# Gathering rows in fp32 and casting them on ScalarE in a gather, cumulative sum and matmul kernel

## The chip, the cores and the metric

The kernel runs on one core of one Trainium2 chip. The metric is the time of one execution on the device, in microseconds; less is better. Before the change it was 410.53 us, the median of three runs (409.6 to 411.24).

The runs of this study fell on several chips, and that turned out to matter. I call them A (the first measurement; which chip it was is not recorded; before takes 410), B (e1, e2, e3, e5 and e9 to e12; before takes 405), C (e4, e6, e7, e8; before takes 411) and D (e13 to e18; before takes **365**). A may be C. The trace of before was taken in an execution of 404.57 us, which fits B's runs of before (404.3 to 407.1 us) and not A's; its chip isn't recorded. Every ratio compares kernels of the same chip.

## The reference

```python
B, S, N, D = 16, 4096, 2048, 512
# x: B x S x D fp32; indices: B x N, sorted, without repeats; w: D x D fp32
gathered = x[b_idx, indices, :]
cs = np.cumsum(gathered, axis=1)
return np.matmul(cs, w).astype(np.float32)
```

## The kernel before

256 tiles of 128 gathered rows run through five stages. GpSimd issues an indirect DMA for a tile. TensorE multiplies the tile with a triangle of ones (`sums`, into `pa`), which gives the sums within the tile, transposed. VectorE adds the last column of the tile before (`carry`, from `pa` to `cst`). TensorE multiplies by w (`project`, into `pb`), ScalarE copies the product to an output buffer (`drain`, from `pb` to `ob`), and a DMA stores it. The lines from the helper that issues a gather:

```python
    NG = 16        # buffers for gathered tiles, R = 2 tiles in one
    def gather(t):
        g, r = divmod(t, R)
        if t % FREE == 0:
            pool.need(s_a, t + FREE - NG)     # TensorE's sums of tile t-16 (and the next) are done
        ...                                   # choose the column of indices
        nc.gpsimd.indirect_dma_start(
            out=g16[g % (NG // R)][:, r, :],  # fp16: the DMA casts
            out_offset=None,
            in_=x_flat,                       # fp32 in HBM
            in_offset=bass.IndirectOffsetOnAxis(ap=ap, axis=0),
            element_offset=(t // NT) * S * D,
        ).then_inc(s_g[t % NS], 16)
...
    for t in range(T):
        gather(t)
        if t % NB == NB - 1:                  # after each fourth tile
            nc.gpsimd.memset(rest[:, t // NB, :], 0.0)   # nobody reads it: 0.54 us of delay
```

```python
    def sums(t, u, first=None):
        ...
        pe.need(s_g[t % NS], ...)             # the tile has landed
        pe.need(s_d, t - NA + 1 - skip, tiles)  # VectorE has emptied pa
        ...                                   # 4 matmuls, then s_a += 1
    def carry(t, first=None):
        dve.need(s_a, t + 1, first)           # TensorE's sums of tile t are done
        ...                                   # add, then s_d += 1
    def drain(u, first=None):
        act.need(s_b, u + 1, first)           # TensorE's product of tile u is done
        nc.scalar.copy(out=ob[...], in_=pb[u % NB][:]).then_inc(s_e, 1)
```

## Time and profile before

| | kernel before, profiled run (404.57 us) |
|---|---|
| span, granted clock | 402.9 us, 0.937 |
| queue q0 (gathers), q1 (stores): share of 16 DMA engines | 58.2%, 43.1% |
| gathers on GpSimd | 256 of 0.94 us |
| gathers in the steady stage | one every 1.478 us |

The lines behind it stand in the prediction below. A page gives for each group the busy time, the mean of one instruction, the idle time ahead of the group on its engine and what ended most of that. A line of the waits gives who waited for what, then the sum in us, how many times, and the longest; "remote" stands where the profile found nobody who had just given the signal.

### The profile page before, as it was taken

The page shows a single profiled execution, that of the slowest core. Times are in us where ns is not written, and L with a number is a line of the kernel's source. Part 1 is how long each engine was busy: PE and PEld are TensorE (multiplying, and loading weights), DVE is VectorE, ACT ScalarE, POOL GpSimd, SP SyncE. Part 2 cuts the span into 40 slices and gives each one's busy share as a digit, 9 for nine tenths or more (in the row PEclk, how much of TensorE's full clock was granted, in tenths as well). Part 3 has the DMA queues.
Part 4 walks back from the last instruction along what each step waited for, and adds up shares of the span by engine and source line. Part 5 has one row for each costly group of instructions (what it writes and reads, how often), then busy time and mean ns, then how long its engine had stood idle before and what let it go on. Part 6 is the DMA issues. An engine that isn't in the chain of part 4 may idle for free.

```text
span 402.9 us, 6104 instructions
## 1 busy us (share of the span) xinstructions
PE 323.7 (80%) x2066; PEld 164.3 (41%) x2066; DVE 178.9 (44%) x263; ACT 144.6 (36%) x260; POOL 277.2 (69%) x330
## 2 busy tenths in 40 slices
PE   7654987978878878978887988889788897787894
PEld 2321443434434433534443434445344453343451
DVE  3311454444444544435444535444444444444561
ACT  2211343333333333333334424333333333333552
POOL 7886777777777777777677777777777767776600
PEclk9886898999999998989989898989999899989998
DMA  7988999999999999999999999999999999999985
GB/s 178 182 119 135 224 247 252 249 248 301 264 237 298 266 243 298 252 295 224 270 297 243 261 279 264 242 289 249 246 295 268 296 212 287 287 225 299 279 321 222
DMA packets 56268, 102.15 MB, mean 254 GB/s; under 512 B 5824, under 2 KB 38848, under 8 KB 56256
## 3 DMA queue, kind: packets, MB, share of 16 engines
q0 software_dynamic: 36864, 33.57, 58.2%
q1 hardware_dynamic: 18832, 67.90, 43.1%
q10 hardware_dynamic: 560, 0.53, 0.4%
q8 instruction: 6, 0.10, 0.1%
q14 instruction: 6, 0.05, 0.0%
HBM read 68.42 MB, written 67.11 MB: 336 GB/s over the span
## 4 chain that ended last, share of the span: by engine, by line
PE 76%; issue 12%; DVE 4%; another core or an unknown queue 2%; DMA 2%; POOL 2%; ACT 1%; DVEq 0%; SPq 0%
PE pb L190 58%; PE pa L145 18%; DVE cst L177 4%; POOL g L125 1%; DMA g<-in_x_dram,idxg 1%; ACT ob L202 1%; DMA idx_first<-in_indices_dram 0%; POOL rest L289 0%; DVEq L26 0%; SPq L411 0%; SPq L92 0%
## 5 line engine op out<-in xcount | busy, mean ns | idle before, releaser
L190 PE MATMUL pb<-w,cst 128*128 128x512 f16 x1024 | 284.0, 401 | 46.0 <-DVE cst L177 23.0
L125 POOL DMA_INDIRECT g<-in_x_dram,idxg x252 | 237.1, 941 | 100.6 <-issue 54.6
L177 DVE TENSOR_TENSOR cst<-pa,cst 128x512 f16<-128x512 f32 x240 | 166.0, 692 | 205.5 <-PE pa L145 163.3
L202 ACT COPY ob<-pb 128x512 f32<-128x512 f32 x256 | 142.0, 590 | 248.3 <-PE pb L190 196.8
L190 PEld LDWEIGHTS pb<-w,cst 128*128 128x128 f16 x1024 | 89.7, 102 | 126.4 <-issue 44.0
L145 PE MATMUL pa<-ut,g 128*128 128x128 f16 x992 | 106.7, 226 | 25.1 <-issue 23.7
L145 PEld LDWEIGHTS pa<-ut,g 128*128 128x128 f16 x992 | 78.0, 102 | 97.9 <-issue 45.9
L289 POOL MEMSET rest<- 128x512 f16 x64 | 34.8, 543 | 0.1
L164 DVE CAST cst<-pa 128x512 f16<-128x512 f32 x16 | 11.0, 685 | 5.5 <-PE pa L145 5.5
L296 PE MATMUL pb<-zeros 128*128 128x512 f16 x16 | 6.0, 542 | 1.5 <-DVE zeros L300 1.5
L125 POOL DMA_INDIRECT g<-in_x_dram,idx_first x4 | 3.9, 987 | 1.6 <-issue 0.9
L296 PEld LDWEIGHTS pb<-zeros 128*128 128x128 f16 x16 | 2.1, 134 | 4.3 <-issue 2.4
L145 PE MATMUL pa<-uq,g 128*128 128x128 f16 x32 | 3.1, 219 | 0.8 <-DMA g<-in_x_dram,idx_first 0.8
L145 PEld LDWEIGHTS pa<-uq,g 128*128 128x128 f16 x32 | 2.4, 97 | 2.7 <-DMA g<-in_x_dram,idx_first 1.0
L303 DVE CAST idxf<-idx 128x128 f32<-128x128 uint32 x2 | 0.5, 228 | 4.1 <-DMA idx<-in_indices_dram 4.1
L366 ACT ACT_TABLE_LOAD x1 | 1.3, 1283 | 2.6 <-issue 2.6
L369 ACT CAST w<-w 128x512 f16<-128x512 f32 x2 | 1.1, 615 | 2.6 <-DMA w<-in_w_dram 2.6
L317 DVE CAST w<-w 128x512 f16<-128x512 f32 x2 | 1.4, 748 | 0.8 <-DMA w<-in_w_dram 0.8
L308 PE MATMUL pb<-ident,idxf 128*128 128x128 f32 x2 | 0.9, 446 | 0.4 <-DVE idxf L303 0.4
L308 PEld LDWEIGHTS pb<-ident,idxf 128*128 128x128 f32 x2 | 0.4, 204 | 1.3 <-DVE idxf L303 1.0
L300 DVE MEMSET zeros<- 128x256 uint32 x1 | 0.3, 272 | 1.1 <-SPq L92 1.1
L314 DVE CAST idxg<-pb 128x128 uint32<-128x128 f32 x2 | 0.6, 288 | 0.4 <-issue 0.4
(11 smaller groups left out, 2.1 us busy)
## 6 DMA issues: line engine op xcount, KB each, us to landing
out_dram<-ob SPq DMA_DIRECT2D x62, 1024.0 KB
g<-in_x_dram,idxg POOLq DMA_INDIRECT x252
out_dram<-ob SPq DMA_DIRECT2D x4, 256.0 KB, 2.8
out_dram<-ob SPq DMA_DIRECT2D x2, 512.0 KB, 3.4
w<-in_w_dram ACTq DMA_DIRECT2D x2, 256.0 KB
w<-in_w_dram SPq DMA_DIRECT2D x2, 256.0 KB
idx<-in_indices_dram SPq DMA_DIRECT2D x2, 128.0 KB, 2.7
g<-in_x_dram,idx_first POOLq DMA_INDIRECT x4
```

Source lines behind the costliest of these rows:

```text
L125: nc.gpsimd.indirect_dma_start(out=g16[g % (NG // R)][:, r, :], out_offset=None, in_=x_flat, in_offset=bass.IndirectOffsetOnAxis(ap=ap, ax ...
L145: mm = nc.tensor.matmul(out=pa[t % NA][:, c], lhsT=g16[g % (NG // R)][:, r, c * P : (c + 1) * P], rhs=uq[:] if g in PLAIN else ut[:], star ...
L164: nc.vector.tensor_copy(out=dst, in_=src).then_inc(s_d, 1)
L177: nc.vector.tensor_tensor(out=dst, in0=src, in1=last, op=mybir.AluOpType.add).then_inc(s_d, 1)
L190: mm = nc.tensor.matmul(out=pb[u % NB][:], lhsT=cst[g % NC][:, c, j, :], rhs=w16[:, c, :], start=(c == 0), stop=(c == DC - 1),)
L202: nc.scalar.copy(out=ob[g // W % NO][:, g % W, j], in_=pb[u % NB][:]).then_inc(s_e, 1)
L289: nc.gpsimd.memset(rest[:, t // NB, :], 0.0)
L296: nc.tensor.matmul(out=pb[NB - 1][:], lhsT=zeros[:, :P], rhs=zeros[:], start=True, stop=True)
L308: nc.tensor.transpose(out=pb[k % NB][:, :P], in_=idxf[:, k, :], identity=ident[:]).then_inc(s_pt, 1)
L317: nc.vector.tensor_copy(out=w16[:, c, :], in_=w32[:, c, :]).then_inc(s_wc, 1)
L366: nc.scalar.copy(out=spare[:], in_=zeros[:, :1])
L369: nc.scalar.copy(out=w16[:, c, :], in_=w32[:, c, :]).then_inc(s_wc, 1)
```

## The change

Intent: on the DMA engines a gathered row that is cast on its way takes longer than a plain one (98 ns at the median for a cast row in the trace of before, 84 for a packet of 2 KB that isn't cast). So gather plain fp32 rows and cast on ScalarE, which is busy for 36% of the time. The clearing after each fourth gather goes. Of each 16th tile the last 8 rows are gathered by an instruction of their own, after the reset that stands in the diff. I meant this to take load off one DMA engine. The first eight pairs of tiles are stored singly.

```diff
-    LEAD = 4
+    LEAD = 3
+    FAR = 6            # casts run up to 6 tiles ahead of the drain
+    NH = 8             # fp16 buffers
...
     def gather(t):
-        if t % FREE == 0:
-            pool.need(s_a, t + FREE - NG)
+        if t >= NG:
+            pool.need(s_c, cast_by[R * (g + 1) - NG - 1])   # ScalarE has cast tile t-16
...
+        parts = [(0, P, ap, s_g[t % NG])]
+        if t % NT == SPLIT:
+            pool.need(s_last, 16)
+            nc.gpsimd.inc_swdge_sem([], [], mode="reset_dge_cursor")
+            parts = [(P - E, P, idx_last[:, t // NT, 0:1], s_h),
+                     (0, P - E, ap[: P - E], s_g[t % NG])]
+        for a, b, ap, done in parts:
+            nc.gpsimd.indirect_dma_start(out=g32[g % (NG // R)][a:b, r, :], ...)
+    def cast(t, n, first=None):
+        for u in range(t, t + n):
+            act.need(s_g[u % NG], ...)
+        nc.scalar.copy(out=g16[...], in_=g32[...]).then_inc(s_c, 1)
...
-    for g in range(W):
+    for g in range(W * NO):
         store(g, 1)
...
-        if t % NB == NB - 1:
-            nc.gpsimd.memset(rest[:, t // NB, :], 0.0)
...                                   # ScalarE's loop: casts, then the drain of tile u
+        for t, n in casts[u if first is None else 2 * U + u]:
+            cast(t if first is None else t - 2 * U, n, first)
         drain(u, first)
```

More of the change, by code (lines that the diff above doesn't have):

```diff
@@ L53 @@
     KI = T // P
+    E = 8
+    SPLIT = NT // 2
     FIRST = 2 * R
     NG = 16
-    NS = 32
-    FREE = 2
-    LEAD = 4
+    LEAD = 3
+    FAR = 6
+    NH = 8
     NA = 4
@@ L64 @@
     U = NT
-    V = NS
-    assert V % NS == 0 and NS % NG == 0 and FREE == R and NS == 16 * R and 2 * U % NS == 0 and (T - 4 * U) % V == 0 and U % (W * R * NO) == 0 and U % NA == 0 and U % (R * NC) == 0 and U % NB == 0
+    V = max(U, W * R * NO)
+    assert U == NT == NG == W * R * NO and V % U == 0 and V % (W * R * NO) == 0 and T % V == 0 and U % NG == 0 and U % NA == 0 and U % (R * NC) == 0 and U % NB == 0
     assert D == 512 and N % (R * P) == 0 and T % P == 0
@@ L74 @@
     idx_first = const.tile([P, FIRST, 2], U32)
+    idx_last = const.tile([E, B, 2], U32)
     idx64 = const.tile([P, KI, 2 * P], U32)
@@ L84 @@
     spare = const.tile([P, 1], FP16)
-    rest = const.tile([P, T // NB, D], FP16)
-    g16 = [const.tile([P, R, D], FP16, name=f"g16_{i}") for i in range(NG // R)]
+    g32 = [const.tile([P, R, D], FP32, name=f"g32_{i}") for i in range(NG // R)]
+    g16 = [const.tile([P, R, D], FP16, name=f"g16_{i}") for i in range(NH)]
     cst = [const.tile([P, DC, R, P], FP16, name=f"cst{i}") for i in range(NC)]
@@ L95, in sem @@
         return tc.alloc_semaphore(name)
-    s_z, s_ut, s_wc, s_if, s_pt, s_prep, s_of, s_c = (
-        sem(f"s_{n}") for n in ("z", "ut", "wc", "if", "pt", "prep", "of", "c")
+    s_z, s_ut, s_wc, s_if, s_pt, s_prep, s_c = (
+        sem(f"s_{n}") for n in ("z", "ut", "wc", "if", "pt", "prep", "c")
     )
@@ L102 @@
     s_idx = [sem(f"s_idx{k}") for k in range(KI)]
+    s_last = sem("s_last")
+    s_h = sem("s_h")
+    s_f = [sem(f"s_f{i}") for i in range(NO)]
     s_ol = sem("s_ol")
-    s_g = [sem(f"s_g{i}") for i in range(NS)]
+    s_g = [sem(f"s_g{i}") for i in range(NG)]
     s_o = [sem(f"s_o{i}") for i in range(NO)]
@@ L113 @@
     )
+    casts = []
+    cast_by = []
+    for u in range(T):
+        far = min(FAR, 2 if u < R else 3 + (u + 4) // 8, 3 + (T - 1 - u) // 6)
+        casts.append([])
+        while len(cast_by) <= min(u + far, T - 1):
+            n = R if far > 5 and len(cast_by) % R == 0 else 1
+            casts[u].append((len(cast_by), n))
+            cast_by += [cast_by[-1] + 1 if cast_by else 1] * n
+    for u in range(2 * U + U, T - 2 * U):
+        assert casts[u] == [(t + U, n) for t, n in casts[u - U]]
     def gather(t):
         g, r = divmod(t, R)
-        if t % FREE == 0:
-            pool.need(s_a, t + FREE - NG)
+        if t >= NG:
+            pool.need(s_c, cast_by[R * (g + 1) - NG - 1])
         if t < FIRST:
@@ L124, in gather @@
             ap = idxg[:, t // P, t % P : t % P + 1]
-        nc.gpsimd.indirect_dma_start(
-            out=g16[g % (NG // R)][:, r, :],
-            out_offset=None,
-            in_=x_flat,
-            in_offset=bass.IndirectOffsetOnAxis(ap=ap, axis=0),
-            element_offset=(t // NT) * S * D,
-        ).then_inc(s_g[t % NS], 16)
-    PLAIN = (0, 1, G - 2, G - 1)
+        parts = [(0, P, ap, s_g[t % NG])]
+        if t % NT == SPLIT:
+            pool.need(s_last, 16)
+            nc.gpsimd.inc_swdge_sem([], [], mode="reset_dge_cursor")
+            parts = [
+                (P - E, P, idx_last[:, t // NT, 0:1], s_h),
+                (0, P - E, ap[: P - E], s_g[t % NG]),
+            ]
+        for a, b, ap, done in parts:
+            nc.gpsimd.indirect_dma_start(
+                out=g32[g % (NG // R)][a:b, r, :],
+                out_offset=None,
+                in_=x_flat,
+                in_offset=bass.IndirectOffsetOnAxis(ap=ap, axis=0),
+                element_offset=(t // NT) * S * D,
+            ).then_inc(done, 16)
+    PLAIN = (0, 1, G - 2, G - 1)
+    def cast(t, n, first=None):
+        g, r = divmod(t, R)
+        for u in range(t, t + n):
+            act.need(s_g[u % NG], 16 * (u // NG + 1), first)
+            if u % NT == SPLIT:
+                act.need(s_h, 16 * (u // NT + 1), first)
+        nc.scalar.copy(
+            out=g16[g % NH][:, r : r + n], in_=g32[g % (NG // R)][:, r : r + n]
+        ).then_inc(s_c, 1)
     def sums(t, u, first=None):
@@ L138, in sums @@
         tiles = None if first is None else R * first
-        skip = 0 if first is None else 2 * U
-        pe.need(s_g[t % NS], 16 * (t // NS + 1) - skip // R, first)
-        pe.need(s_d, t - NA + 1 - skip, tiles)
+        pe.need(s_c, cast_by[t] if first is None else cast_by[2 * U + t] - 2 * U // R, first)
+        pe.need(s_d, t - NA + 1, tiles)
         for c in range(DC):
             if c == 1 and u is not None:
-                pe.need(s_e, u - NB + 1 - skip, tiles)
+                pe.need(s_e, u - NB + 1, tiles)
             mm = nc.tensor.matmul(
                 out=pa[t % NA][:, c],
-                lhsT=g16[g % (NG // R)][:, r, c * P : (c + 1) * P],
-                rhs=uq[:] if g in PLAIN else ut[:],
+                lhsT=g16[g % NH][:, r, c * P : (c + 1) * P],
+                rhs=uq[:] if first is None and g in PLAIN else ut[:],
                 start=(c == 0),
@@ L183, in project @@
         tiles = None if first is None else R * first
-        skip = 0 if first is None else 2 * U
-        pe.need(s_e, u - NB + 1 - skip, tiles)
-        pe.need(s_d, (u + 1 if g in PLAIN else R * (g + 1)) - skip, tiles)
+        pe.need(s_e, u - NB + 1, tiles)
+        pe.need(s_d, u + 1 if first is None and g in PLAIN else R * (g + 1), tiles)
         for c in range(DC):
             if c == 2 and t is not None:
-                pe.need(s_d, t - NA + 1 - skip, tiles)
+                pe.need(s_d, t - NA + 1, tiles)
             mm = nc.tensor.matmul(
@@ L206, in store @@
         rows = out[b, h * R * P : (h + n) * R * P, :]
-        src = ob[g // W % NO]
+        i = g // W % NO
+        src = ob[i]
+        done = s_ol if g >= G - W else s_f[i] if 0 < g < W * NO and g % W else s_o[i]
         if g in (0, G - 1):
@@ L210, in store @@
                 sp.need(s_e, R * g + j + 1)
-                done = s_ol if g else (s_o[0], s_of)[j]
                 nc.sync.dma_start(
                     out=rows[j * P : (j + 1) * P, :], in_=src[:, g % W, j]
-                ).then_inc(done, 16)
+                ).then_inc(s_f[0] if j and not g else done, 16)
             return
         sp.need(s_e, R * (g + n))
-        done = {1: s_of, G - W: s_ol}.get(g, s_o[g // W % NO])
+        order = "(g j p) d -> p g j d" if g in PLAIN else "(g p j) d -> p g j d"
         nc.sync.dma_start(
-            out=rows.rearrange(
-                "(g j p) d -> p g j d" if g in PLAIN else "(g p j) d -> p g j d", p=P, j=R
-            ),
-            in_=src[:, g % W : g % W + n],
+            out=rows.rearrange(order, p=P, j=R), in_=src[:, g % W : g % W + n]
         ).then_inc(done, 16)
@@ L234 @@
             ).then_inc(s_first[k], 16)
+        nc.scalar.dma_start(
+            out=idx_last[:],
+            in_=indices[:, (SPLIT + 1) * P - E : (SPLIT + 1) * P]
+            .bitcast(U32)
+            .rearrange("b (p w) -> p b w", w=2),
+        ).then_inc(s_last, 16)
     idx_rows = indices.bitcast(U32).rearrange("b (t q) -> (b t) q", q=2 * P)
@@ L242 @@
         eng.dma_start(out=w32[:, c, :], in_=w[c * P : (c + 1) * P, :]).then_inc(s_w[c], 16)
-    for g in range(W):
+    for g in range(W * NO):
         store(g, 1)
-    for g in range(W, G - W, W):
+    for g in range(W * NO, G - W, W):
         store(g, W)
@@ L341 @@
     tail = order.index((False, T - 2 * U - 1)) + 1
-    step = 2 * V
+    step = 2 * U
     for i in range(head + step, tail):
-        assert order[i] == (order[i - step][0], order[i - step][1] + V)
+        assert order[i] == (order[i - step][0], order[i - step][1] + U)
     def run(i, first=None):
@@ L348, in run @@
         after = next((v for k, v in order[i + 1 :] if k != is_sums), None)
+        if first is not None:
+            t -= 2 * U
+            after -= 2 * U
         if is_sums:
@@ L356 @@
         run(i)
-    with nc.tensor.Fori(2 * U // R, (T - 2 * U) // R, V // R) as first:
+    with nc.tensor.Fori(2 * U // R, (T - 2 * U) // R, U // R) as first:
         pe.new_pass()
@@ L371, in step @@
         if u % (W * R) == 0:
-            if first is None and u == W * R * NO:
-                act.need(s_of, 16 * (R + W - 2))
-            act.need(s_o[u // R // W % NO], 16 * (u // R // W // NO), first)
+            i, slot = divmod(u // (W * R), NO)
+            if first is None and i == 1:
+                act.need(s_f[slot], 16 * (W - 1 + (slot == 0) * (R - 1)))
+            act.need(s_o[slot], 16 * i, first)
+        for t, n in casts[u if first is None else 2 * U + u]:
+            cast(t if first is None else t - 2 * U, n, first)
         drain(u, first)
@@ L379 @@
         step(u)
-    with nc.scalar.Fori(2 * U, T - 2 * U, U) as first:
+    with nc.scalar.Fori(2 * U, T - 2 * U, V) as first:
         act.new_pass()
-        for u in range(U):
+        for u in range(V):
             step(u, first)
```

## The prediction

> **What bounds the kernel now.** I read the page first: the slices, the DMA queues, the HBM line.
>
> ```profile
> PE   7654987978878878978887988889788897787894
> POOL 7886777777777777777677777777777767776600
> DMA  7988999999999999999999999999999999999985
> q0 software_dynamic: 36864, 33.57, 58.2%
> q1 hardware_dynamic: 18832, 67.90, 43.1%
> HBM read 68.42 MB, written 67.11 MB: 336 GB/s over the span
> ```
>
> The DMA digit is 9 from the fifth slice to within 20 us of the end, and the two queues together took 101% of what 16 engines have. PE is at 7 to 9. q0 is the gathers (32768 rows and 4096 semaphore writes), q1 the stores. Next, the steady stage alone: the windows, limited to the tile g, so the POOL column counts gathers and nothing else.
>
> ```profile
> 10.00:50.00 40.00, 8.01 (x72) 6.35 (x72) 26.35 (x28) 0.79 0.88 164
> 50.00:350.00 300.00, 88.08 (x816) 63.47 (x816) 190.63 (x203) 0.95 1.06 265
> ```
>
> (Columns: window, length, PE, weight loads, POOL, each busy us and count, granted clock, DMA share, GB/s.) 203 gathers in 300 us is **1.478 us per tile** of 128 rows; 256 tiles at that rate are 378 us. The other 402.9 - 378 = 25 us is start and tail; from 10 to 50 us only 28 gathers were issued, at a lower clock and DMA share.
>
> Is it really DMA? The groups, the waits and the timeline say what the others need per tile.
>
> ```profile
> L190 PE MATMUL pb<-w,cst 128*128 128x512 f16 x1024 | 284.0, 401 | 46.0 <-DVE cst L177 23.0
> L202 ACT COPY ob<-pb 128x512 f32<-128x512 f32 x256 | 142.0, 590 | 248.3 <-PE pb L190 196.8
> L289 POOL MEMSET rest<- 128x512 f16 x64 | 34.8, 543 | 0.1
> L369 ACT CAST w<-w 128x512 f16<-128x512 f32 x2 | 1.1, 615 | 2.6 <-DMA w<-in_w_dram 2.6
> ...
> ACT ob L202 <- remote: 43.3, 22, 4.3
> POOL g L125 <- PE pa L145: 23.1, 38, 1.4
> POOL g L125 <- remote: 22.9, 17, 2.5
> ...
> 10.19 0.94 POOL L125 DMA_INDIRECT g<-in_x_dram,idxg  x1 [0.30 <-issue]
> 11.44 0.94 POOL L125 DMA_INDIRECT g<-in_x_dram,idxg  x1 [0.30 <-issue]
> 12.68 0.94 POOL L125 DMA_INDIRECT g<-in_x_dram,idxg  x1 [0.30 <-issue]
> 13.61 0.55 POOL L289 MEMSET rest<- 128x512 f16 x1
> 14.32 0.95 POOL L125 DMA_INDIRECT g<-in_x_dram,idxg  x1 [0.17 <-issue]
> 386.83 0.58 PEld L190 LDWEIGHTS pb<-w,cst 128*128 128x128 f16 x4
> 386.89 1.03 PE L190 MATMUL pb<-w,cst 128*128 128x512 f16 x4
> 387.97 1.03 PE L190 MATMUL pb<-w,cst 128*128 128x512 f16 x4
> ```
>
> POOL unhindered issues a gather every 11.44 - 10.19 = 1.245 us; with the memset after each fourth, four tiles take 14.32 - 8.94 = 5.38 us (8.94 is the start of the gather before these rows), 1.345 us each. So it is only 9% faster than the 1.478 us that the stage runs at, and it waited 46 us for buffers. PE at full clock does a tile in 387.97 - 386.89 = 1.08 us; VectorE's add takes 0.69. ACT waited 43 us for something remote: its output buffers, which stores must empty. Each engine is faster than 1.478 and held up by buffers that transfers free: **the DMA engines bound the steady stage**.
>
> The transfer records, one by one, size it. A gathered row (2 KB read, 1 KB written as fp16) takes 98 ns at the median, the semaphore write behind it 22; a 4 KB store packet 159 to 172; a 2 KB packet that isn't cast (the weights, and stores of 2 KB runs) **84**. Per tile and engine: 8 x 98 + 22 for the gather, 4 x 161 for the store, about 5 for the store's semaphores: 1.455 us, 98.4% of 1.478. Some 1,600 gather rows took 150 ns to over 1 us (the mean is 112), which is why shares add to more than one; they overlap packets of the other queue.
>
> [...]
>
> **The change, part by part.**
> Gathers in fp32: each row is a plain 2 KB packet, I take 84 ns for 98. Per tile and engine 8 x 14 = 112 ns less. HBM traffic is the same; SBUF writes double. 1.478 - 0.112 = 1.366 us per tile, times 256 = 349.7 us, **28.7 us less**. This is on the bounding resource, so it counts in full while nothing else takes more than 1.366.
>
> Casts on ACT: in the loop one instruction of 1024 columns per pair[...]; a drain is 0.59[...]. Beside other work, except at the start and the end, where a cast of 615 ns is one more link: +1 to +2 us. The order of instructions shows ACT casting six tiles ahead of its drain, and a gather waiting for the cast of the tile 16 before it, about what sums gave before.
>
> Memsets gone: POOL falls to 1.245 us per tile.
>
> Split of tile 8 of each 16: one more gather of 8 rows and one cursor reset on POOL. If these cost together 1.0 us (an estimate: the 0.30 gap[...]), 1.245 + 1.0/16 = 1.31 us per tile. Still under 1.366, barely. [...]
>
> First eight pairs stored singly: stores start earlier in a stage where the DMA has gathers only (121 and 128 GB/s from 20 to 40 us). I take 2 to 3 us off, against the added casts.
>
> Sum: 349.7 + 25 (start and tail) - 2.5 + 1.5 = 373.7, rounded down to 372.5[...]. Runs without a profile were 410.53 - 402.9 = 7.6 us longer than this span: **380 us**, 7.4% less.
>
> **The rivals.**
> (a) POOL becomes the bound. If the reset and the small gather cost 3 us and more a time[...], POOL needs 1.43 us per tile and up: 366 us + start 3 + tail 12 + 7.6 = 389. For it: POOL is within 9% now, and nothing in the trace prices the reset. Against: only 16 of them.
> (b) A 2 KB packet saves nothing beside stores: HBM reads and writes together must rise from 2 x 262144 B / 1.478 us = 355 GB/s to 384, and the write side of SBUF doubles for gathers. If rows still took 98 ns, the time would be 408. Against: 98 is the cast's own time, as weight rows of the same 2 KB took 84; and in the transfer view of 200 to 250 us single slices of 1.25 us, with stores in them, moved 401 to 410 GB/s.
> (c) ACT becomes a coupling: casts stand in order behind drains that wait for stores, and gathers wait for casts. A stall of 4 us (the longest above) then stops gathers too. Against: 16 buffers are over 20 us of gathers, and the DMA has stores to move in just those stalls. I'd give it 3 to 8 us.
> (d) The slow start shortens by far more than I take: up to 10 us, giving 370.
>
> **Range and chances.** The centre 380 has the cast saving in full; (c) and (a) in mild forms reach 390 to 396[...]. Range 368 to 396. Within 2% means over 402.3: that takes (b), or (a) in a severe form. Faster 0.91, same 0.06, slower 0.03.
>
> **What would show it.** Right: gather packets of 2 KB near 84 ns, q0's share of the engines falling from 58% to about 50% of a shorter span, gathers every 1.36 us in the steady stage, DMA still at 9[...]. Wrong: DMA below 9 with POOL's waits gone (a); rows near 98 ns (b); POOL waiting long for ACT's casts while DMA digits fall to 8 (c). The whole is wrong if a reset takes microseconds or if the stores' packets lengthen as the gathers' shorten.

The sum came to 349.7 + 25 - 2.5 + 1.5 = 373.7 us of span; I put it at 372.5 for a small gain by the split, and 7.6 us more gave 380. Of the 1.0 us for the reset and the small gather only the gap of 0.30 us is from the trace; the rest was my guess. That the casts fit beside other work can be put from the trace alone: a cast of 512 columns took 615 ns and a drain 590, so one of each per tile makes about 1.21 us, under 1.366 (an estimate).

## The result

The changed kernel took **471.25 us** (median of four runs, 467.16 to 475.28), beside 410.06 for before: ratio 1.1455 (95% interval 1.1353 to 1.1557), **slower**. The result is correct. A ratio is the mean time of one kernel's fast runs over that of the other's of the same rounds, so not quite the ratio of the medians. The profiled run of the changed kernel (475.28 us, span 473.3) counts as slow, as it lies 1.7% above the fastest; its granted clock of 0.873 is that of the fast runs (0.872 to 0.874).

The page of the changed kernel, slices and queues, to be held against those in the prediction:

```profile
PE   6408783875887687678678587587769747758595
POOL 7756556464655745566545565557566555665200
DMA  7766878787988978798878898798799888888756
q0 software_dynamic: 20992, 67.13, 44.1%
q1 hardware_dynamic: 18880, 67.90, 36.7%
HBM read 68.42 MB, written 67.11 MB: 286 GB/s over the span
```

The DMA digit fell from 9 to 7 and 8, and GpSimd's from 7 to 5 and 6. q0 did fall, from 58.2% of 403 us to 44.1% of 473: the engines have less to do, yet everything takes longer. The windows say the same of the steady stage (columns: window, length, then PE, weight loads, ACT and POOL with counts, for tile g alone; granted clock, DMA share, GB/s):

```profile
50.00:350.00 300.00, 74.01 (x692) 57.59 (x692) 92.59 (x92) 174.46 (x184) 0.87 0.84 299
```

184 gather instructions in 300 us where before had 203, some of them the small ones. Groups and waits of the changed kernel:

```profile
L154 POOL DMA_INDIRECT g<-in_x_dram,idxg x252 | 240.4, 954 | 141.4 <-issue 71.0
L154 POOL DMA_INDIRECT g<-in_x_dram,idx_last x16 | 14.4, 899 | 37.4 <-ACT g L171 33.6
L171 ACT CAST g<-g 128x1024 f16<-128x1024 f32 (+1 forms) x147 | 138.9, 948 | 0.3 <-issue 0.2
```

```profile
ACT ob L239 <- PE pb L227: 104.0, 78, 4.2
POOL g L154 <- ACT g L171: 104.1, 42, 5.2
ACT ob L239 <- remote: 82.1, 24, 11.5
```

GpSimd waits 104 us for ScalarE's casts, 42 times, up to 5.2 us at once. A gather of 8 rows takes 899 ns and one of 128 rows 954: the price is per instruction, not per row. GpSimd's timeline shows the rhythm:

```profile
212.63 0.95 POOL L154 DMA_INDIRECT g<-in_x_dram,idxg  x1 [0.30 <-issue]
213.89 0.95 POOL L154 DMA_INDIRECT g<-in_x_dram,idxg  x1 [0.30 <-issue]
215.14 0.95 POOL L154 DMA_INDIRECT g<-in_x_dram,idxg  x1 [0.31 <-issue]
217.87 0.95 POOL L154 DMA_INDIRECT g<-in_x_dram,idxg  x1 [1.78 <-ACT g L171]
```

Several gathers at 1.25 us each, then a pause; the one shown ended when a cast did. ScalarE's timeline there, from TensorE's signal on: a drain, then the cast, which ends at 217.60 us.

```profile
216.07 0.59 ACT L239 COPY ob<-pb 128x512 f32<-128x512 f32 x1 [2.00 <-PE pb L227]
216.55 1.05 ACT L171 CAST g<-g 128x1024 f16<-128x1024 f32 x1
```

**Where the time went.** I worked out an account of GpSimd's stream from the records of the traces: the gathers' own time, the clearings, the gaps below 0.45 us between instructions (issue), the longer pauses, and what remains of the span after the last gather. (The record of a cursor reset can lie inside a gather's; it is left out here, as it would cut a gap in two.) These rows are fast runs, but for the last.

| kernel (chip) | gathers | busy | clearing | small gaps | pauses (number, us) | after the last gather | span |
|---|---|---|---|---|---|---|---|
| before (not recorded) | 256 | 241.1 | 34.8 | 60.1 | 35, 41.4 | 23.0 | 402.9 |
| e4, before without clearings (C) | 256 | 240.6 | 0 | 62.1 | 51, 79.0 | 23.0 | 407.9 |
| e5, plain rows, no casts (B) | 256 | 242.6 | 34.9 | 60.1 | 34, 40.2 | 22.7 | 403.2 |
| e7, e5 with the split (C) | 272 | 258.6 | 34.9 | 66.4 | 32, 47.3 | 22.8 | 432.5 |
| e2, change without the split (B) | 256 | 243.1 | 0 | 66.0 | 39, 99.1 | 27.1 | 438.5 |
| changed kernel (A, slow run) | 272 | 258.8 | 0 | 68.0 | 49, 111.7 | 31.6 | 473.3 |

(All begin near 3.2 us, and with that each row adds up to its span within 1 us.) From before to the changed kernel: 70.3 us more of pauses, 25.6 us for 16 more gathers and their gaps, 8.6 us more at the end, and 34.8 us less of clearing: 69.7 of the 70.4 us. By the medians the loss is 61 us; the traces are of a fast execution of before (404.57 us) and a slow one of the changed kernel (475.28 us).

One sum hardly moves. Clearings and pauses together are 76.2 us in before. By the same account they are 75.1, 74.4, 74.6 and 75.1 in e5, e10, e11 and e12, the runs without casts on B, and 79.0, 81.4 and 82.2 in e4, e6 and e7, those on C. There a clearing only takes the place of a pause, while each further gather adds itself. With gathers that wait for casts the sum is larger (99.1 in e2, 111.7 in the changed kernel). On D it is 35.3 in e13 and nothing in e17.

**Why the stream pauses at all.** The trace of before holds part of it, and I had not looked. TensorE's and then VectorE's timeline of the kernel before, in the steady stage; only TensorE's `sums` groups, which VectorE waits for, are kept:

```profile
108.16 0.39 PE L145 MATMUL pa<-ut,g 128*128 128x128 f16 x4
...
109.24 0.39 PE L145 MATMUL pa<-ut,g 128*128 128x128 f16 x4
...
110.33 0.39 PE L145 MATMUL pa<-ut,g 128*128 128x128 f16 x4
...
111.42 0.39 PE L145 MATMUL pa<-ut,g 128*128 128x128 f16 x4
```

```profile
109.32 0.69 DVE L177 TENSOR_TENSOR cst<-pa,cst 128x512 f16<-128x512 f32 x1 [0.79 <-PE pa L145]
110.77 0.69 DVE L177 TENSOR_TENSOR cst<-pa,cst 128x512 f16<-128x512 f32 x1 [0.75 <-PE pa L145]
112.92 0.69 DVE L177 TENSOR_TENSOR cst<-pa,cst 128x512 f16<-128x512 f32 x1 [1.46 <-PE pa L145]
115.78 0.69 DVE L177 TENSOR_TENSOR cst<-pa,cst 128x512 f16<-128x512 f32 x1 [2.17 <-PE pa L145]
```

TensorE's records come 1.09 us apart, VectorE's starts 1.45, 2.15 and 2.86 us: VectorE falls behind, though it is idle and waits for TensorE. The records of the semaphore say that it was not VectorE that was late: s_a rises about 0.02 us ahead of each of VectorE's starts.

Counted from the later of TensorE's recorded end and the end of VectorE's own instruction before, VectorE's starts lag by 198 us in sum over the 256 tiles (a first count, used in the expectations, said 220).

So in this trace the signal that VectorE waits for comes after TensorE's recorded end of the sums, so counted by up to 5 us. But it can't all be late work: s_a was recorded rising at 117.25, 117.36 and 117.48 us, for three tiles in 0.23 us, and 60 of its 242 recorded steps take less than 0.4 us, where a tile takes TensorE 1.08. So at least part of the delay is in the signals: they are held back and come through together. What holds them back no run shows. "Late finishes" below means this.

GpSimd, which waits for the same late signals, then pauses until several arrive (s_a rises 2 or 3 times in each of the 35 pauses of before's trace):

```profile
113.95 0.95 POOL L125 DMA_INDIRECT g<-in_x_dram,idxg  x1 [0.17 <-issue]
115.20 0.94 POOL L125 DMA_INDIRECT g<-in_x_dram,idxg  x1 [0.30 <-issue]
117.50 0.94 POOL L125 DMA_INDIRECT g<-in_x_dram,idxg  x1 [1.37 <-remote]
```

The pause before the gather at 105.68 us ended the same way: 8 gathers and their two clearings in 117.50 - 105.68 = 11.82 us, the 1.478 us per tile that the prediction took for the DMA engines' pace.

### The profile page after: what moved, and what is told of

Its sections match the earlier page's. It is cut to its first block, busy times and chain, and to the rows that moved or that the text cites. A ratio compares the mean times of both kernels' runs of the same rounds, so it can differ in the third digit from the quotient of the medians.

```text
span 473.3 us, 6449 instructions
## 1 busy us (share of the span) xinstructions
PE 334.0 (71%) x2066; PEld 172.7 (36%) x2066; DVE 178.6 (38%) x263; ACT 263.7 (56%) x407; POOL 260.3 (55%) x282
## 3 DMA queue, kind: packets, MB, share of 16 engines
q0 software_dynamic: 20992, 67.13, 44.1%
## 4 chain that ended last, share of the span: by engine, by line
PE 68%; another core or an unknown queue 11%; DVE 9%; issue 8%; ACT 2%; DMA 1%; SPq 0%; DVEq 0%; ACTq 0%
PE pb L227 50%; PE pa L183 17%; DVE cst L215 9%; ACT ob L239 1%; DMA w<-in_w_dram 1%; ACT g L171 0%; DVE cst L202 0%; ACT w L412 0%; SPq L279 0%; DVEq L26 0%; SPq L265 0%; ACTq L26 0%; SPq L457 0%; SPq L95 0%
## 5 line engine op out<-in xcount | busy, mean ns | idle before, releaser
L227 PE MATMUL pb<-w,cst 128*128 128x512 f16 x1024 | 295.8, 416 | 119.0 <-DVE cst L215 96.8
L154 POOL DMA_INDIRECT g<-in_x_dram,idxg x252 | 240.4, 954 | 141.4 <-issue 71.0
L239 ACT COPY ob<-pb 128x512 f32<-128x512 f32 x256 | 146.0, 594 | 198.3 <-PE pb L227 104.0
L227 PEld LDWEIGHTS pb<-w,cst 128*128 128x128 f16 x1024 | 94.8, 105 | 201.3 <-DVE cst L215 103.6
L171 ACT CAST g<-g 128x1024 f16<-128x1024 f32 (+1 forms) x147 | 138.9, 948 | 0.3 <-issue 0.2
L183 PEld LDWEIGHTS pa<-ut,g 128*128 128x128 f16 x992 | 82.2, 105 | 83.7 <-issue 26.2
L154 POOL DMA_INDIRECT g<-in_x_dram,idx_last x16 | 14.4, 899 | 37.4 <-ACT g L171 33.6
```

The lines of the kernel that those rows point to most:

```text
L154: nc.gpsimd.indirect_dma_start(out=g32[g % (NG // R)][a:b, r, :], out_offset=None, in_=x_flat, in_offset=bass.IndirectOffsetOnAxis(ap=ap, ...
L171: nc.scalar.copy(out=g16[g % NH][:, r : r + n], in_=g32[g % (NG // R)][:, r : r + n]).then_inc(s_c, 1)
L183: mm = nc.tensor.matmul(out=pa[t % NA][:, c], lhsT=g16[g % NH][:, r, c * P : (c + 1) * P], rhs=uq[:] if first is None and g in PLAIN else ...
L227: mm = nc.tensor.matmul(out=pb[u % NB][:], lhsT=cst[g % NC][:, c, j, :], rhs=w16[:, c, :], start=(c == 0), stop=(c == DC - 1),)
L239: nc.scalar.copy(out=ob[g // W % NO][:, g % W, j], in_=pb[u % NB][:]).then_inc(s_e, 1)
```

## The experiments

Theories: **D**, the DMA engines bound the kernel (the prediction's); **G** and **P**, GpSimd's stream of gathers with its pauses for TensorE's late finishes sets the pace; **C**, the casts cost by ScalarE's time (C1) or by the wait for them that they put before a gather (C2); **S**, the split costs by its extra instructions; **L**, the lead of 3 in place of 4.

### e1: the change with the clearings back

```diff
     for t in range(T):
         gather(t)
+        if t % NB == NB - 1:
+            nc.gpsimd.memset(rest[:, t // NB, :], 0.0)
```

> The changed kernel with the memset after every fourth gather put back. In both profiles VectorE and ScalarE learn of finished matmul groups 2 to 9 us late while GpSimd issues gathers one after another, and the late ones arrive together when GpSimd pauses. Theory P (pacing): the memsets were pauses that let these through; putting them back takes the time from 471 to 430 us or less, and the longest lag of VectorE behind PE from 10 us to about 5. Theory C (casts on ScalarE couple gathers to drains): no change, 465 to 475. Theory S (split) and theory L (lead of 3): no change.

462.85 us (459.55 to 465.47), ratio 1.1382 (1.1303 to 1.1461), chip B. The clearings don't mend it. Nor did leaving them out do the harm: pauses in the account are 72.3 us with 34.8 us of clearings, 100.9 in e3 without.

### e2: the change without the split

```diff
-            nc.gpsimd.inc_swdge_sem([], [], mode="reset_dge_cursor")
-            parts = [(P - E, P, idx_last[...], s_h), (0, P - E, ap[: P - E], s_g[t % NG])]
```

> The changed kernel with the 16 split gathers back to one gather of 128 rows each, and no cursor reset. Theory S (the split costs, by its extra gathers of 0.90 us and waits at the reset): 16 times 2 to 3 us, so 471 goes to 425 to 440. Theory P: 16 gathers fewer in a row, some 1.2 us each at most, 455 to 468. Theories C and L: within 1% of 471.

442.3 us (435.45 to 447.7), chip B; two of four runs were slow, and the two fast ones (440.24 and 435.45) over before's 405.5 make 1.080. So the split is 23 to 28 us of the loss, the rest about 32 us. (That is e1 and e3 against this; the changed kernel itself did not run on B, and these two differ from it by the clearings and the lead.) The waits of e2:

```profile
POOL g L149 <- ACT g L164: 96.6, 38, 5.6
```

### e3: the change with the old lead

```diff
-    LEAD = 3
+    LEAD = 4
```

> The changed kernel with PE running its sums four tiles ahead as before, not three. Theory L (three tiles of 1.09 us hide only 3.3 us of a late finish, four hide 4.4): 471 falls to 440 or less. Theories P, C, S: 462 to 475, a gain of at most 2%.

465.53 us (457.84 to 474.24), ratio 1.1475 (1.1404 to 1.1545), chip B. Two of its four runs count as slow; the fast ones took 457.84 and 463.63, 1.136 of before's 405.5. L falls: it asked for 440 or less.

### e4: before without the clearings

```diff
-        if t % NB == NB - 1:
-            nc.gpsimd.memset(rest[:, t // NB, :], 0.0)
```

> The kernel before without its memsets, nothing else. Accounts of the gather stream so far: 256 gathers of 0.94 us, gaps of 0.30, 35 us of memsets and some 35 pauses of 1.35 us, in which GpSimd waits for buffers; the same account holds to 1 us with plain fp32 rows. Late finishes of PE reach VectorE and ScalarE some 1.05 us after the last gather has been issued. Theory G (the gather stream on GpSimd is the bound, and its pauses are set by when PE's finishes come through): without memsets the stream loses 35 us and the pauses grow by less than that, so 375 to 398. Theory P (the memsets let finishes through): 410 or more, with pauses of 80 us and over.

409.81 us, ratio 0.9976 (0.993 to 1.0022), chip C: the same. 34.8 us of work leave GpSimd, and its pauses grow from 41.4 to 79.0 us (of the growth up to 6 us may be the chip, as before takes 404.57 us in its trace and 411 on C). The stream isn't bound by GpSimd's own work there; it waits for something that takes its time anyway.

### e5: before with plain fp32 rows, without casts

```diff
-    ut = const.tile([P, R, Q], FP16)
+    ut = const.tile([P, R, Q], BF16)      # uq likewise
-    g16 = [const.tile([P, R, D], FP16, ...
+    g16 = [const.tile([P, R, D], FP32, ...
-                lhsT=g16[g % (NG // R)][:, r, c * P : (c + 1) * P],
+                lhsT=g16[g % (NG // R)][:, r, :].bitcast(BF16)[:, 2 * c * P + 1 : 2 * (c + 1) * P : 2],
```

TensorE reads the upper half of each fp32 number as bf16; the result is within tolerance.

> The kernel before with fp32 gathers and no cast anywhere: PE reads the upper 16 bits of each fp32 as bf16, so the result is off by bf16 truncation, on purpose. Memsets, waits and lead are as before. It shows what plain rows do to the time by themselves. My prediction's step (a plain row takes 84 ns for 98, and the DMA engines bound): 375 to 385 us. If plain gathers themselves are what slows (longer packets beside the stores, or more delay for PE): 420 or more. Theory C (the casts): 375 to 412 here, as nothing waits for ScalarE.

404.92 us (404.72 to 406.41), ratio 0.9991 (0.9954 to 1.0028), chip B. This is the prediction's main step alone, and it saves nothing. The queues, and the windows for tile g with the columns as in the prediction:

```profile
q0 software_dynamic: 20480, 67.13, 50.3%
q1 hardware_dynamic: 18832, 67.90, 42.1%
```

```profile
200.00:250.00 50.00, 13.85 (x134) 10.12 (x135) 32.19 (x34) 1.00 0.98 355
250.00:300.00 50.00, 14.36 (x135) 9.93 (x135) 31.70 (x34) 1.00 0.96 356
300.00:350.00 50.00, 14.20 (x134) 9.93 (x133) 31.82 (x35) 1.00 0.97 355
```

The gathers' share fell by 8 points, as predicted, and the pace stayed at 103 gathers in 150 us, 1.46 us each. The granted clock is 1.00 in all three, so the late finishes aren't the clock that these records show either.

### e6: e5 with casts on ScalarE that nothing waits for

```diff
+        if u % R == 0:
+            nc.scalar.copy(out=dst16[u // R % 8][:], in_=src32[:])   # 1024 columns per pair, fixed source
```

> The kernel with plain rows and no cast, plus one ScalarE copy of 1024 fp32 columns to fp16 for each pair, from a fixed tile, for which nothing waits. It separates ScalarE's time from the waits through it. Theory C1 (a drain that comes later behind a copy keeps PE and GpSimd waiting): 420 to 440. Theory C2 (only gathers that wait for a cast cost): 403 to 412.

410.87 us, ratio 1.0 (0.9956 to 1.0044), chip C. ScalarE's time (C1) costs nothing. That leaves the wait for the casts as the cost; this is by elimination, and the single stores of the first pairs were never tried alone.

### e7: e5 with the split

```diff
+        if t % NT == SPLIT:
+            pool.need(s_last, 16)
+            nc.gpsimd.inc_swdge_sem([], [], mode="reset_dge_cursor")
+            parts = [(P - E, P, idx_last[:, t // NT, 0:1], s_h), (0, P - E, ap[: P - E], s_g[t % NS])]
```

> The kernel with plain rows and no cast, plus the split of every 16th tile with its cursor reset. An 8-row gather took 0.90 us in the changed kernel against 0.94 for 128 rows, so 16 more cost 16 x 1.2 = 19 us if the gather stream bounds (theory G): 420 to 428. Theory D (the DMA engines bound and one of them is the slowest): 395 to 404, faster than without the split. If the split also desynchronizes more than that: 430 and over.

436.67 us (434.16 to 437.45), ratio 1.0636 (1.0589 to 1.0683), chip C: against e5's 0.9991 S alone costs 6.45% of 405 to 411, 26 us. The spans of e5 and e7, of two chips, differ by 29.3 us; by the account 16.0 of these are the 16 gathers themselves, 6.1 their gaps, and 7.1 longer pauses, about the 6 us by which before itself differs between the two chips. So nearly all that the split costs is the time of its instructions.

### e8: e2 with the casts up to 10 tiles ahead

```diff
-    FAR = 6
+    FAR = 10
-        far = min(FAR, 2 if u < R else 3 + (u + 4) // 8, 3 + (T - 1 - u) // 6)
+        far = min(FAR, 2 if u < R else 3 + (u + 4) // 4, 3 + (T - 1 - u) // 4)
```

> The changed kernel without the split, with casts ten tiles ahead of their drains instead of six. A gather then waits for a cast that stands four tiles earlier in ScalarE's order. Theory C2 (the pauses end only after ScalarE has worked through drains to the cast): pauses fall from 99 us to 60 or less and 442 goes to 400 to 415. Theory C1 (ScalarE's order delays drains): 442 or worse. Theory P (PE's finishes come through only when gathers pause): less pausing but the same time, 435 to 445.

450.31 us (448.44 to 450.75), ratio 1.0945 (1.089 to 1.1), chip C: earlier casts don't help.

### e9 and e10: 32 buffers, for e2 and for before

```diff
-    NG = 16
+    NG = 32
```

(e9 also counts ScalarE's loop in pairs of tiles, for the longer ring.)

> The change without the split (442.3 us with 16 fp32 buffers, 438.5 us in its profile, pauses of the gather stream of 99 us) with 32 fp32 buffers, so that a gather waits for a cast that lies 32 tiles back, not 16. Theory W (the wait that came with the change is the cost: a gather waits for a cast, which stands behind drains that wait for TensorE's late finishes): the wait of the gathers on the casts (96.6 us) shrinks, and the time falls by at least half of the 32 us that it lies over before, to 410 to 426. Rival P (TensorE's finishes are told to the other engines only when the gather stream pauses, so the pauses are needed, however many buffers there are): 432 to 448 us, pauses of 85 to 110 us, the same wait told at another place of the ring.

> The kernel before with 32 gather buffers of fp16 in place of 16, nothing else changed. Theory P (the gather stream and the pauses that it needs set the pace): within 1.5% of before, pauses of the stream of 35 to 50 us as before. Rival B (the kernel before lacks buffers: gathers wait because a buffer comes free late, and issued earlier they would fill the gaps): 385 to 398 us, pauses under 20 us.

e9: 453.97 us, ratio 1.1194 (1.1122 to 1.1265); e10: 420.4 us, ratio 1.0376 (1.0333 to 1.0418); both chip B. More buffers make both kernels slower. e10's pauses stay (32, 39.5 us) and its last gather ends at 378.7 us, where before's ended at 379.9: the stream keeps its pace, and only TensorE has 32 tiles left in place of 16, 40 us of tail in place of 23. Theory W, that a longer ring takes away the wait for the casts, falls: the gathers of e9 wait 95.8 us for them, those of e2 96.6.

### e11: before with half as many clearings of twice the length

```diff
-        if t % NB == NB - 1:
-            nc.gpsimd.memset(rest[:, t // NB, :], 0.0)              # 512 columns
+        if t % (2 * NB) == 2 * NB - 1:
+            nc.gpsimd.memset(rest[:, t // (2 * NB), :], 0.0)        # 1024 columns
```

> The kernel before with its 64 clearings of 512 columns gathered into 32 of 1024 columns, one after each eighth gather: the same total of 35 us of clearing, in pauses of about 1.1 us plus issue. Theory P (a pause of the gather stream of 1.1 us or more lets the late finishes through): the natural pauses (35 of them, 41 us) mostly vanish, and the time falls to 375 to 395 us. Rival H (how the pause is cut up makes no difference: the pauses come because a group of tiles takes as long as it takes): 404 to 415 us, natural pauses of 35 to 50 us as before.

408.46 us (406.29 to 411.33), ratio 1.007 (0.9994 to 1.0145), chip B. Clearings twice as long don't make the natural pauses vanish (32, 43.5 us): that part of theory P, a pause of 1.1 us as a cure, falls.

### e12: e5 with rows of 128 bytes

```diff
+    Z = 32
+    x_short = x.rearrange("b s (k z) -> (b s k) z", z=Z)
-            out=g16[g % (NG // R)][:, r, :],
+            out=g16[g % (NG // R)][:, r, :Z],
-            in_=x_flat,
+            in_=x_short,
```

> Wrong result on purpose. Plain fp32 gathers without casts, as in the run that took 404.9 us, but each row is cut to its first 32 numbers (128 of 2048 bytes), so gathers have as many instructions, rows and packets' starts but a sixteenth of the bytes; the rest of the buffers holds ones. Theory G (the issue of the gathers on GpSimd and what it does to TensorE's finishes set the pace, not the bytes): 395 to 408 us. Theory D (the DMA engines bound the kernel, as predicted): the share of q0 falls from 50% to under 20% and the time to 350 us or less.

411.94 us (411.05 to 414.55), ratio 1.0188 (1.0131 to 1.0245), chip B, unclear by the limit of 2%; wrong result on purpose. Its first gather starts at 10.0 us where before's starts at 3.2, as the buffers are first filled with ones: that is 6.8 of the 7.3 us. Its slices, queue and steady stage:

```profile
DMA  4123054465465365464564554454465545655575
q0 software_dynamic: 8192, 4.21, 6.5%
```

```profile
50.00:350.00 300.00, 87.63 (x817) 63.33 (x817) 0.00 (x0) 192.20 (x204) 0.96 0.52 187
```

**A sixteenth of the bytes, fewer packets too (8192 for e5's 20480), the DMA engines half idle, and 204 gathers in 300 us, where before had 203.** On B theory D is out.

### e13: before with 8 buffers

```diff
-    NG = 16
+    NG = 8
```

> The kernel before with 8 gather buffers in place of 16. Theory T (the rate of the steady stage doesn't hang on the ring's depth, which only sets how much is left for TensorE when the gathers have ended; 32 buffers cost 15.8 us, about 16 tiles of 1 us): 8 fewer buffers save 6 to 9 us, 396 to 401 us where before takes 405, last gather ends near 380 us. Rival N (8 tiles of prefetch are too few, gathers wait for buffers more often and TensorE for data): 415 us or more.

365.91 us (365.4 to 366.57) beside 364.94: ratio 1.0032 (1.001 to 1.0053). This was chip D, where **before itself** takes 365 us, so theory T went untested, but the profile shows what is different there. The waits of e13, then its gathers:

```profile
ACT ob L202 <- PE pb L190: 201.5, 256, 4.2
DVE cst L177 <- PE pa L145: 161.6, 238, 2.4
```

```profile
L125 POOL DMA_INDIRECT g<-in_x_dram,idxg x252 | 237.2, 941 | 68.5 <-issue 61.9
```

VectorE waits 161.6 us for TensorE, as long as in before's trace (163.3 us), but in 238 waits where that had 122: nearly one with each tile, and 2 of 257 steps of s_a take less than 0.4 us. Its lag over all tiles sums to 9.9 us, not 198. GpSimd, busy as long as there, hardly pauses (once, 0.6 us), and its stream ends at 347.9 us. And D shows once more how little a DMA share of 1 says; the windows of e13 for tile g:

```profile
50.00:330.00 280.00, 81.33 (x830) 58.32 (x831) 195.33 (x209) 0.99 1.12 292
```

The same cast gathers at 1.34 us each and a share of **1.12**. The prediction took 1.06 for a full load.

### e14, e15 and e18, e16: what the gathers do to the chain

```diff
# e14: only the first 16 tiles are gathered; all later tiles read those buffers
-    for t in range(T):
+    for t in range(NG):
         gather(t)
# e15, and e18 the same again: memsets from tile 16 on
+            nc.gpsimd.memset(fill[t % 2][:], 0.0).then_inc(s_c, 1)   # 896 columns
# e16: from tile 16 on the gathers land in buffers that nobody reads
-            out=g16[g % (NG // R)][:, r, :],
+            out=(g16 if t < NG else away)[g % (NG // R)][:, r, :],
```

> Wrong result on purpose. Only the first 16 tiles are gathered and all later tiles read those 16 buffers again; no clearings. The chain of TensorE, VectorE, ScalarE and the stores stays. Theory I (the gathers on GpSimd slow the chain): 1.1 to 1.2 us a tile, 295 to 330 us in all, and the waits of VectorE on TensorE (163 us before) fall below 60. Rival K (the chain itself takes 1.48 us a tile): 390 us or more.

> Wrong result on purpose. As the run with only 16 gathers, but GpSimd keeps the pace of the kernel before: a memset of about 0.94 us in the place of each gather, waiting for the same buffers, and the clearings. Theory I (gathers, not GpSimd work as such, delay what is told of TensorE's groups): 310 to 345 us, set by GpSimd at 1.3 us a tile or by TensorE. Rival J (any work on GpSimd that waits on TensorE does it): 390 to 410 us.

> Wrong result on purpose. As before, with all 256 gathers, clearings and the gathers' waits, but from tile 16 on they land in buffers that nobody reads, and TensorE reads the first 16 buffers again without a wait. Theory I (the issue of the gathers itself delays the chain): 390 to 408 us. Rival A (data arriving late hold TensorE): 345 us or less, set by GpSimd's 1.3 us a tile.

> Wrong result on purpose; memsets in place of the gathers after the first 16. On a chip where before takes 405 to 411 us. Theory I (VectorE's lag behind TensorE comes only where gathers are issued): 300 to 320 us, lags in sum under 20 us where before shows 220. Rival J (any work on GpSimd that waits on TensorE brings the lag, or that chip's TensorE is slow anyway): 360 us or more. On a chip where before takes 365 us: 301 us again, nothing new.

Wrong results on purpose. All fell on D. e14: 301.01 us, e15: 300.75, e18: 300.64, with TensorE busy for the whole of 50 to 280 us in each: the chain of TensorE, VectorE, ScalarE and stores needs about 1.09 us per tile when it doesn't wait for gathers. e16: 395.53 us, ratio 1.0831, but its lags sum to 9.8 us and TensorE is done with all tiles by 300 us; from there on the gathers run on alone, so its total says nothing about the chain. As D has no lag to begin with, theories I and J stay undecided.

e16 does say something about the DMA engines of D. Its page:

```profile
POOL 7777888777875766576666666664666778788770
DMA  7999999999999999999999999999999977777771
L128 POOL DMA_INDIRECT away<-in_x_dram,idxg x240 | 225.8, 941 | 103.5 <-DMA away<-in_x_dram,idxg 50.1
```

With stores every 1.09 us beside them, the gathers go out only every 1.66 us between 100 and 300 us, and wait 50.1 us for the landing of earlier ones: there the DMA engines are the bound, at a share that stays at 1.11 in each 50 us of it. So a bound by DMA exists on D, and full load reads about 1.11 there. e13 with 1.12 runs close to it, though its GpSimd hardly waits.

### e17: the changed kernel on D

No edit.

> The changed kernel itself, once more. On a chip where before takes 405 to 411 us: 455 to 475 us, as measured. On a chip where before takes 365 us. Theory G (there the gather stream on GpSimd, 1.24 us an instruction, sets the pace; the clearings, 35 us, are gone and 16 more gathers cost 20 us): 345 to 358 us, so faster than before. Rival W (the waits of gathers on casts cost as much there): 380 us or more.

**362.35 us** (362.08 to 363.07) beside 365.09: ratio 0.9935 (0.9916 to 0.9954), the same within 2%. Its gathers, its wait for the casts, and its steady stage:

```profile
L154 POOL DMA_INDIRECT g<-in_x_dram,idxg x252 | 239.9, 952 | 76.8 <-issue 71.0
L154 POOL DMA_INDIRECT g<-in_x_dram,idx_last x16 | 14.3, 896 | 4.9 <-issue 4.9
```

```profile
POOL g L154 <- ACT g L171: 5.8, 19, 0.3
```

```profile
50.00:330.00 280.00, 81.96 (x837) 60.09 (x837) 110.20 (x105) 212.03 (x224) 0.99 1.01 391
```

The wait of 104 us has shrunk to 5.8, in gaps of 0.3 us at most. 224 gathers in 280 us is 1.25 us each: GpSimd's bare rate, with no time for anything else. The account: 258.2 busy, 82.6 small gaps, no pause, against e13's 241.2, 34.7 of clearing, 68.8 and 0.6. So on D the change takes out 34.7 us of clearing and puts 17 + 14 us of further gathers and gaps in its place. G's 345 to 358 us missed by 4; its pace of 1.24 us an instruction was right.

## Why the prediction was wrong

It said 380 us (368 to 396); it was 471.25.

**The step that failed is "the DMA engines bound the steady stage".** It rested on three things. One was that packet times sum to 98.4% of 1.478 us, and the shares to 1.06. That isn't full load: e13 reaches a share of 1.12 on chip D with the same packets, and e12 runs at the old pace with a share of 0.52. The second was elimination: each engine is faster than 1.478 us and waits, so transfers must hold them. But TensorE's 1.08 us was read from the matmuls' records and not from the signals that the others wait for, and at a moment (387 us) when the gathers were over. Among gathers its signals come at a median of 1.49 us (s_a in before's trace), in bursts. The third was a misreading: "ACT waited 43 us for something remote: its output buffers, which stores must empty". The semaphore records of that trace show that each of these 22 waits ended with s_b, TensorE's signal, more than 1.5 us after TensorE's recorded end, and the 17 remote waits of GpSimd with s_a. None of them ended with a store.

The 28.7 us put on this step measured 0 (e5: ratio 0.9991).

A sum was wrong as well: 410.53 - 402.9 = 7.6 us is no cost outside the span, but the difference of two executions. The one with the span of 402.9 us took 404.57, so 1.7 us lie outside it. This is small beside the miss.

**Plain rows at 84 ns for 98** was right in the small: in the trace of the changed kernel the fp32 rows travel two to a packet of 4096 bytes, 159 ns at the median, 79.5 a row. It shortened what nobody waited for.

**Casts on ScalarE**: one of 1024 columns took 1.05 us; as work they cost nothing (e6: ratio 1.0). **Rival (c)**, that they couple the gathers to the drains, was right in kind and far too small: "3 to 8 us" became about 33 us (ratio 1.080 for e2 against 0.9976 for e4, before without clearings). Its reason, that 16 buffers are over 20 us of gathers, fails because the stream comes to the end of the ring every 8 or so gathers whatever its length (e9, e10: 32 buffers, as many pauses). At each pause before goes on 0.3 us after the finishes arrive; the changed kernel needs a drain and a cast of 1.05 us first. e2 pauses 99.1 us in sum, e4 79.0; its small gaps, the gathers and the tail after the last one bring the rest. This reading of the 33 us is argued from e3, e5 and e6, in which the lead, the plain rows and ScalarE's time cost nothing; no run takes out the wait alone.

**The split**: I took 1.0 us for each; the small gather is 0.90 and its gap 0.30, the reset itself 28 ns in the records. This part of the arithmetic holds: 16 x 1.2 = 19 us of GpSimd's time, and the account on D leaves room for no more. On A to C the split cost 26 us by e7. No gain from it was seen in any run. What the reset does to the DMA engines isn't shown either; on D (e17) the record of each reset lies 6 to 10 gathers ahead of its small gather.

**Clearings gone** was right as a saving of GpSimd's time (34.8 us) and wrong in value on A to C: pauses take their place (e4), as the sum of clearings and pauses stays at 74 to 82 us.

Together on A to C: 33 us for waiting on casts and some 26 us for the split, 59 of the 60 us that 14.55% of 410 make.

On D the stream of gathers is the bound, as rival (a) had it in name, by 1.25 us an instruction and not by a slow reset, and the change comes out 0.65% ahead.

**What stays open.** Why TensorE's signals come late and in bursts among gathers on A to C and not on D (VectorE's lags sum to 198 us in before's trace, to 9.9 in e13). It isn't the bytes (e12), the granted clock in the records (e5: 1.00), the casts or the clearings (e4, e5). It is gone in the last 20 us, when no more gathers are issued: from 380 to 400 us the lags of e10 sum to 1.0 us over 19 tiles, while 20 us of its steady stage (from 80 us on) have 9 to 13. That points to the gathers, and so does the nearly fixed sum of clearings and pauses, but the runs made to prove it fell on D. No version that beats before on A to C was found; on D the change without split and clearings should need 256 x 1.25 + 19 = 339 us, an estimate from e17's pace and tail that was not run.

## What to carry to other kernels

A DMA share near 1 is a sum of packet times and no proof of a bound (1.06 in before was none; full load in e16 read 1.11): ask for the same number of instructions with a sixteenth of the bytes before building on it. See which semaphore ended a wait before giving it to somebody. Compare when an engine's finish is recorded with when its consumer starts; where those drift apart (VectorE's lag in before's trace: up to 5 us), a "fast" engine is not free, and a new consumer in that chain (here a cast between finish and next gather) pays the wait at every turn. And run the kernel before on more than one chip: one change was 14.6% slower on one and 0.7% faster on another.
